# First operands of a hybrid encoder block: the norm chain contiguous, input tiles kept, VectorE in GpSimd's place, units in pairs

## The chip, the cores and the metric

The kernel runs on one core of one Trainium2 chip. The metric is the device time of one execution in microseconds (us), the median of several runs. Engines carry the names of the profile: PE is TensorE, PEld its weight loads, DVE VectorE, ACT ScalarE, POOL GpSimd, SP the engine that issues all DMAs.

## The reference, cut to what matters

One layer, 1024 tokens of width 1024. The piece at the start of the program is `h = rms_norm(x) * (1 + scale) + shift`, where shift and scale come from the vector c by a matrix product, and then `h @ w_in`, a product with many column blocks.

```
shift, scale, gate = adaln(c, w_ada_mix[i], b_ada_mix[i])      # silu(c) @ w + b, split in 3
h = rms_norm(x, norm_mix_w[i]) * (1.0 + scale) + shift
x = x + gate * mixer_sublayer(h, w_in[i], ...)
...
def mixer_sublayer(h, w_in, ...):
    proj = h @ w_in
    conv_in, z, xbc, dt_raw, g_conv, g_ssm = jnp.split(proj, splits, axis=-1)
    a_half, b_half = jnp.split(conv_in, 2, axis=-1)
    u = causal_depthwise_conv(a_half * jax.nn.sigmoid(b_half), conv_dw_w, conv_dw_b)   # 31 taps
    u = jax.nn.silu(layer_norm(u, ...)); y_conv = u @ w_conv_out
    ...                                                        # SSD scan over xbc and dt
    merged = jax.nn.sigmoid(g_conv) * y_conv + jax.nn.sigmoid(g_ssm) * y_ssm
    return merged @ w_out
```

A SwiGLU FFN with a norm of its own and a last norm follow.

## The kernel before

**Layout.** Channels lie on the 128 partitions, tokens along the free dimension. The 1024 tokens are two halves of 512, so a tile is 128x512. Half 0 of h has eight channel tiles `H[0..7]`. Each float32 operand is split in a high part (rounded, ACT) and a low part (the rest, by a subtraction on DVE or POOL), `Hh`/`Hl` and `wh`/`wl`, and each product is three matmuls: high by high, high by low, low by high.

**Start.** `x0` are the eight tiles of half 0. ACT squares them and DVE adds (`SumSq`, names sax and sqx); PE sums over channels (scx, `tokcols`); `rsqrt` makes the reciprocal root r_x in 12 small DVE instructions; `bcast` spreads it over the partitions with matmuls (bx) and an ACT copy (bcx). Beside it `ada` makes shift and scale: for each of eight channel tiles two tiles of 128x1024 (wa_m) are loaded and DVE reduces each against c (an instruction of 1024 columns with a read of the accumulator behind it); `make_h` then multiplies x by gain and root, adds the shift (ACT, `Hh`) and makes `Hl` (DVE).

**Six gates.** `gate0(m)`, m from 0 to 5, are plain products of a weight block with all eight tiles of H: 8 x 3 = 24 matmuls of 512 columns each, into the PSUM tiles p. Gates 0 to 3 run ahead of the step `begin`, gates 4 and 5 behind it.

**Units.** The rest of `proj` is made for both halves at once by a Strassen-Winograd scheme: a unit takes two column blocks, splits seven weight combinations a to g (the splits are named ap0h, ap0l, bp0h, ... by letter and number of the unit), and runs seven products of 12 matmuls each. X is made of a, d, f, g, Y of b, Z of c and e; the PSUM tiles are uXp, uYp, uZp. Its right sides are made from H (half 0) and from the normed tiles of half 1 by `tok_ops`: T1, T2, B22, T3, T4, four tiles of each. That needs the half-1 norm (a second chain scx, r_x, bx, bcx), a scaling of the eight tiles x1t (L883) and whole tiles of h for half 0, which `whole` (L833) adds together again on POOL as Hh + Hl. `Unit.first` runs products a and b, `Unit.rest` c to g. `run_units` decides the order: with A_HEAD = 3 the firsts of units 0, 1, 2, then the rests of 0 and 1, and from there a first and a rest in turn. The table `ENG_A` says for each unit which of its eleven VectorE-like operations go to DVE ("v") and which to POOL ("g"): for unit 0 nine of eleven on DVE, for all others all on POOL.

**Queues.** Instructions are traced in program order and placed by a scheduler; on each engine they run in the order in which they were placed, and a waiting instruction holds up all behind it. `issue_after` forces instructions behind a given one on that one's engine. `tick` feeds background work (31-tap convolutions on DVE as `conv31`, the dt chain `dt_part`) between matmuls. SP issues the DMAs in its own order. `pstile` gives one of four PSUM tiles, `mmtile` one of three, `xtile` one of these or the one in pool cv.

Of the kernel before, what the change touches and what calls it, by code (L numbers as in the profile page):

```python
# [6 lines left out]
F32 = mybir.dt.float32  # L7
# [7 lines left out]
P = 128  # L15
T = 512
# [7 lines left out]
NCK = 4  # L24

NWADA = 8
ROW_AT = 3
A_HEAD = 3
FF_HEAD = 6
FF_TAIL = 2  # L30
G_BOTH = (0, 3)
# [14 lines left out]
N_G0 = 8  # L46
PRI_W = 300

ENG_A = ("ggvvvvvvvvv", "ggggggggggg")
ENG_F = ("vvvvvvvgggg",) * 6 + ("ggvgvgvgvvv",)  # L50
ENG_D = ("vvvvvvvgggg",)
EPS = 1e-6
# [19 lines left out]
def build(tc, ins, outs):  # L72
# [83 lines left out]
    def split_w_(w, ch, nk, eng, alloc=None):  # L156

        parts = []
        for q in range(0, nk, 4):
            n = min(4, nk - q) * P  # L160
            raw = w[:, q * P:q * P + n]
            alloc = alloc or (lambda tag, name: wpool.tile([P, 4 * P], F32R, tag=tag, name=name))
            hi = alloc("whi", f"wh{ch}_{q}")
            act(out=hi[:, :n], in_=raw, func=AF.Copy)  # L164
            lo = alloc("wlo", f"wl{ch}_{q}")
            eng.tensor_tensor(out=lo[:, :n], in0=raw, in1=hi[:, :n].bitcast(F32), op=ALU.subtract)  # L166
            parts.append((hi, lo))
        return parts

    def mm3(out, w, slots, rhs, first=True, last=True, after=None):  # L170

        n = len(slots)
        for i, (s, (rh, rl)) in enumerate(zip(slots, rhs)):
            whi, wlo = w[s // 4]
            sl = slice(s % 4 * P, (s % 4 + 1) * P)
            if i % 2:
                tick()
            ins = after(i) if after else None
            with tc.issue_after(ins) if ins else nullcontext():
# [7 lines left out]
    def xtile(i, name):  # L187

        return pools["cv"].tile([P, T], F32, tag="cv", name=name, bufs=1) if i % 4 == 3 else mmtile(name)
# [74 lines left out]
    def rsqrt(st, scale, eps, name, out=None):  # L264

        v, t = small("v" + name), small("t" + name)
        r = out if out is not None else small("r" + name)
        vec.tensor_scalar(out=v, in0=st, scalar1=scale, scalar2=eps, op0=ALU.mult, op1=ALU.add)
        vec.tensor_scalar(out=r.bitcast(I32), in0=v.bitcast(I32), scalar1=1, scalar2=None,
                          op0=ALU.logical_shift_right)  # L270
        vec.tensor_scalar(out=r.bitcast(I32), in0=r.bitcast(I32), scalar1=-1, scalar2=0x5F3759DF,
                          op0=ALU.mult, op1=ALU.add)
        for _ in range(3):
            vec.scalar_tensor_tensor(out=t, in0=r, scalar=-0.5, in1=r, op0=ALU.mult, op1=ALU.mult)
            vec.tensor_tensor(out=t, in0=t, in1=v, op=ALU.mult)
            vec.scalar_tensor_tensor(out=r, in0=t, scalar=1.5, in1=r, op0=ALU.add, op1=ALU.mult)
        return r

    nrow = [0]
# [54 lines left out]
    def make_h(k, t, gcol, shift, r, eng, dst=H, keep=None):  # L334
        vec.scalar_tensor_tensor(out=t, in0=t, scalar=gcol[:, k:k + 1], in1=r, op0=ALU.mult, op1=ALU.mult)
        hi, lo = dst[k]
        act(out=hi, in_=t, func=AF.Identity, bias=shift[:, k:k + 1])
        if keep is not None:
            act(out=keep, in_=t, func=AF.Identity, bias=shift[:, k:k + 1])
        if eng is vec:  # L340
            vec.scalar_tensor_tensor(out=lo, in0=t, scalar=shift[:, k:k + 1], in1=hi.bitcast(F32),  # L341
                                     op0=ALU.add, op1=ALU.subtract)
        else:
            act(out=t, in_=t, func=AF.Identity, bias=shift[:, k:k + 1])
            gp.tensor_tensor(out=lo, in0=t, in1=hi.bitcast(F32), op=ALU.subtract)

    mod_m = const.tile([P, 24], F32, name="mod_m")
    mod_f = const.tile([P, 24], F32, name="mod_f")
# [527 lines left out]
    def norm_of(b2, r, g, sh, gp_from=KD, fold=False):  # L876

        def scaled(k):
            if k >= gp_from:
                act(out=b2[k], in_=b2[k], func=AF.Copy, scale=g[:, k:k + 1])  # L880
                gp.tensor_tensor(out=b2[k], in0=b2[k], in1=r, op=ALU.mult)
            else:
                vec.scalar_tensor_tensor(out=b2[k], in0=b2[k], scalar=g[:, k:k + 1], in1=r,  # L883
                                         op0=ALU.mult, op1=ALU.mult)
        return scaled, sh, fold
# [259 lines left out]
    def phase_a():  # L1145
        def z_done(i):
            def f(t, src, m, hf):
                act(out=t, in_=src, func=AF.Silu)
                dma(out=z_d[hf, i + m], in_=t)
            return f  # L1150

        def g_done(q, i):
            def f(t, src, m, hf):
                act(out=t, in_=src, func=AF.Tanh, scale=0.5)
                dma(out=gt_d[hf, q, i + m], in_=t)
            return f

        ci = [(CH_CI + 2 * i, CH_CI + 2 * i + 1, ConvIn(i)) for i in range(KD)]
        gates = [((CH_GC, CH_GS)[q] + i, (CH_GC, CH_GS)[q] + i + 1, Each(f"g{q}{i}", g_done(q, i)))
                 for q in range(2) for i in range(0 if q else N_GATE, KD, 2)]  # L1160
        zs = [(CH_Z + i, CH_Z + i + 1, Each(f"z{i}", z_done(i))) for i in range(0, 16, 2)]
        rest = [u for p in zip(gates, zs) for u in p] + zs[len(gates):]
        ssm = [(CH_G + 6 * g + q, CH_G + 6 * g + q + 1, SsmIn(g, q)) for g in G_BOTH for q in range(0, 6, 2)]
        for n, u in enumerate(ssm):
            rest.insert(G_AT + n * G_STEP, u)
        units = []
        while rest or ci:
            if ci and len(units) in CI_AT:
                units.append(ci.pop(0))
            else:  # L1170
                units.append(rest.pop(0))


        def gate0(m):
            def f(w):
                pt = xtile(m, f"p0_0{m}")
                mm3(pt, w, W8, H, after=None if m < 4 else
                    (lambda k: bcast.last if m > 4 or k >= ROW_AT else None))
                t = mp.tile([P, T], F32, tag="x0", name=f"ga{m}", bufs=2)
                act(out=t, in_=pt, func=AF.Tanh, scale=0.5)  # L1180
                dma(out=gt_d[0, 0, m], in_=t)
            step(f, CH_GC + m)

        def begin(_):
            popen("a1", "a1")
            pools.update(u=mp, nev=6, nfr=2, nfs=1)
            pt = [pools["c"].tile([P, NH * T + CW - 1], F32, tag="u", name=f"t1_{k}", bufs=2) for k in range(2)]
            t1 = [pt[k // 2][:, k % 2 * T:(k % 2 + 1) * T] for k in range(4)]
            for _ in tok_ops(pools["a1"], x1t, t1, norm_of(x1t, r_row, gmix, mod_m[:, 0:8])):
                pass  # L1190

        for m in range(4):
            gate0(m)
        step(begin)
        set_drains((bg_dt, 1), (bg_conv_a, CONV_RATE))
        for m in range(4, N_GATE):
            gate0(m)

        def dt1(_):
            bg_dt.append(dt_part(0, ev, [(k, H[k]) for k in range(KD)]))  # L1200

        run_units("p", units, A_HEAD, 0, (False, ()), engs_a, None, {5: [dt1]})


    def phase_b():
# [400 lines left out]

    def xtok(n, k):
        if n == 0:
            t = ap0.tile([P, T], F32, name=f"x0_{k}")
        else:  # L1610
            t = mp.tile([P, T], F32, tag="ev" if k < 6 else "g0", name=f"x1_{k}", bufs=6 if k < 6 else 2)
        dma(out=t, in_=xT[n, :, k, :])
        return t
# [7 lines left out]
        return half_w.pop(0)  # L1621

    def late_w(tag, name):
        return ap0.tile([P, T], F32R, tag="w", name=name, bufs=4)

    x0, x1t = [], []
    ss = SumSq("x0", eng=vec)
# [3 lines left out]
    silu_c(ap0.tile([P, KD * P], F32, tag="wada", name="ctmp", bufs=NWADA))  # L1631
    a = ada(ap0, wada_mix, range(8), mod_m, gmix, "m", True)
    r = bcast(ss.rstd(1.0 / 1024, EPS, out=r_x[0]), "x0", far=False)
    for b in range(KD):
        next(a)
        make_h(b, x0[b], gmix, mod_m[:, 0:8], r, vec)
        if b < 4:
            ch, nk, eng = chunks[b][:3]
            raws.append(load_w_(ch, nk) if b < 2 else ap0.tile([P, 8 * P], F32, name=f"w{ch}"))
            if b > 1:  # L1640
                dma(out=raws[b], in_=wall[ch])
            parts.append(split_w_(raws[b], ch, nk, gp, (None, None, early_w, late_w)[b]))
    ss = SumSq("x1", eng=vec, of=KD)
    for k in range(KD):
        with tc.issue_after(wa_last[0]):
# [108 lines left out]
```

## Time and profile before

| what | value |
|---|---|
| time before, median of 3 runs | 2137.74 us (2136.13 to 2140.61) |
| profiled execution, its own time | 2132.49 us |
| its span, first to last instruction | 2130.5 us |
| PE busy | 1954.8 us, 92% |
| DVE busy | 1561.3 us, 73% |
| POOL busy | 1168.1 us, 55% |
| ACT busy | 964.2 us, 45% |
| mean granted clock | 0.967 |

The profiled execution is 5.2 us under the median, and 2.0 us of it lie outside the span. A busy share is a mean over the whole span; what a stage waits for is read from that stage.

### The profile page before, as it was taken

To read this page: it belongs to the slowest core of one execution; us is meant where nothing else is said; L and a number is where in the kernel's file an instruction comes from. 1 tells how busy PE (TensorE), PEld (TensorE's weight loads), DVE (VectorE), ACT (ScalarE), POOL (GpSimd) and SP (SyncE) were. 2 spreads that over 40 slices of the span, in tenths; PEclk is the share of its full clock that TensorE was granted. 3 is DMA by queue.
4 is the path that set the end of the run, shared out by engine and by line. 5 is a ranking of instruction groups with operands and counts; after the bars stand their busy time and mean duration, and the time that the engine had idled before them with its cause. 6 is when DMAs were issued, how large, how long until landed. Compare 5 with 4: busy or idle time off the path is not lost.

```text
span 2130.5 us, 26723 instructions
## 1 busy us (share of the span) xinstructions
PE 1954.8 (92%) x8802; PEld 1554.5 (73%) x8802; DVE 1561.3 (73%) x2242; ACT 964.2 (45%) x1792; POOL 1168.1 (55%) x871
## 2 busy tenths in 40 slices
PE   4879999999998889898989899998999999989997
PEld 3668678787876666676767677776888888767776
DVE  8868889958899878959779783758644444598645
ACT  3534444444444747446344653346333333444243
POOL 4568678887885854585655764555333333331410
PEclk9889999999999989999999999999999999999998
DMA  8223132322323967689788786863422222576553
GB/s 321 80 70 113 68 102 84 119 104 74 109 102 135 302 201 247 201 301 290 242 277 271 246 260 218 275 229 109 149 99 77 77 84 89 180 255 215 190 187 119
DMA packets 163818, 365.94 MB, mean 172 GB/s; under 512 B 18728, under 2 KB 19168, under 8 KB 163680
## 3 DMA queue, kind: packets, MB, share of 16 engines
q1 hardware_dynamic: 163680, 364.25, 51.2%
q8 instruction: 69, 1.13, 0.2%
q14 instruction: 69, 0.57, 0.1%
HBM read 281.04 MB, written 83.13 MB: 171 GB/s over the span
## 4 chain that ended last, share of the span: by engine, by line
PE 53%; DVE 23%; DMA 13%; issue 4%; ACT 3%; POOL 3%; SPq 1%; DVEq 0%; POOLq 0%; ACTq 0%
PE uXp L805 12%; PE uXf L805 10%; PE uZp L805 6%; PE uZf L805 5%; PE uYp L805 3%; PE uYf L805 2%; DMA M<-acs_d 2%; PE uXd L805 2%; DMA wa_f<-in 2%; DMA yl<-y_d 1%; DVE wa_m L242 1%; DVE wa_f L242 1%; DVE Hl L211 1%; PE uZd L805 1%; PE fd L180 1%
## 5 line engine op out<-in xcount | busy, mean ns | idle before, releaser
L166 POOL TENSOR_TENSOR wl<-w,wh 128x512 fp32r<-128x512 f32 x198 | 283.4, 1440 | 226.6 <-ACT wh L164 185.6
L164 ACT ACTIVATE wh<-w 128x512 fp32r<-128x512 f32 x232 | 136.8, 606 | 135.4 <-DMA w<-in 60.1
L918 POOL TENSOR_TENSOR fw<-fw,fw 128x512 f32<-128x512 f32 x40 | 58.0, 1450 | 117.5 <-DMA fw<-in 116.8
L548 ACT ACTIVATE M<-M,dt_acs 128x128 f32<-128x128 f32 x256 | 81.0, 390 | 45.2 <-DMA M<-acs_d 45.0
L553 POOL TENSOR_TENSOR M<-M,cbm 128x512 f32<-128x512 f32 x48 | 69.4, 1456 | 44.4 <-ACT M L550 25.9
L660 DVE SCALAR_TENSOR_TENSOR pcM<-u,cw_eo,pcM 128x512 f32<-128x512 f32 x120 | 90.3, 752 | 2.7
L660 DVE SCALAR_TENSOR_TENSOR pcQ<-u,pc,pcQ 128x512 f32<-128x512 f32 x112 | 84.4, 754 | 3.0
L182 PE MATMUL s<-Hh,wl 128*128 128x512 f32 x192 | 77.8, 406 | 3.0 <-POOL wl L166 3.0
L660 DVE SCALAR_TENSOR_TENSOR pcR<-u,pc,pcR 128x512 f32<-128x512 f32 x104 | 78.4, 754 | 2.8
L181 PE MATMUL s<-Hl,wh 128*128 128x512 f32 x192 | 77.1, 401 | 2.5 <-DVE Hl L211 2.5
L180 PE MATMUL s<-Hh,wh 128*128 128x512 f32 x192 | 77.3, 406 | 0.5 <-ACT wh L164 0.5
L916 POOL TENSOR_TENSOR fsf<-fw 128x512 f32<-128x512 f32 x22 | 41.2, 1873 | 65.3 <-DVE cf2l L784 10.8
L180 PE MATMUL p<-Hh,wh 128*128 128x512 f32 x144 | 59.0, 430 | 19.1 <-DVE xo L1097 10.8
L180 PE MATMUL p<-Oh,wh 128*128 128x512 f32 x144 | 60.6, 421 | 8.4 <-DVE xo L1097 8.4
L181 PE MATMUL p<-Hl,wh 128*128 128x512 f32 x144 | 60.7, 423 | 5.9 <-DVE Hl L341 5.9
L985 DVE TENSOR_TENSOR s2f<-s2f,uZf 128x512 f32<-128x512 f32 x22 | 15.1, 687 | 62.5 <-PE uZf L805 62.5
L181 PE MATMUL p<-Ol,wh 128*128 128x512 f32 x144 | 60.0, 417 | 0.0
L182 PE MATMUL p<-Oh,wl 128*128 128x512 f32 x144 | 59.5, 414 | 0.0
L925 POOL TENSOR_TENSOR fw<-fw 128x512 f32<-128x512 f32 x40 | 58.6, 1466 | 1.5
L182 PE MATMUL p<-Hh,wl 128*128 128x512 f32 x136 | 56.8, 418 | 0.0
L1094 DVE SCALAR_TENSOR_TENSOR p<-pre,pc,p 128x512 f32<-128x512 f32 x72 | 53.9, 748 | 0.8 <-ACT p L1090 0.2
L180 PE MATMUL wo<-Oh,wh 128*128 128x512 f32 x128 | 51.6, 403 | 0.0
(3620 smaller groups left out, 6973.7 us busy)
## 6 DMA issues: line engine op xcount, KB each, us to landing
fw<-in SPq DMA_DIRECT2D x133, 512.0 KB, 3.4
w<-in SPq DMA_DIRECT2D x100, 512.0 KB, 4.9
M<-acs_d SPq DMA_DIRECT2D x64, 256.0 KB, 6.1
wa_f<-in SPq DMA_DIRECT2D x48, 256.0 KB, 3.5
wa_m<-in SPq DMA_DIRECT2D x16, 512.0 KB, 10.2
xs<-xbc_d SPq DMA_DIRECT2D x32, 256.0 KB, 5.0
E<-eac_d SPq DMA_DIRECT2D x64, 128.0 KB, 6.1
y<-z_d SPq DMA_DIRECT2D x32, 256.0 KB, 5.2
```

Source lines behind the costliest of these rows:

```text
L164: act(out=hi[:, :n], in_=raw, func=AF.Copy)
L166: eng.tensor_tensor(out=lo[:, :n], in0=raw, in1=hi[:, :n].bitcast(F32), op=ALU.subtract)
L180: nc.tensor.matmul(out=out, lhsT=whi[:, sl], rhs=rh, start=first and i == 0, stop=False)
L181: nc.tensor.matmul(out=out, lhsT=whi[:, sl], rhs=rl, start=False, stop=False)
L182: nc.tensor.matmul(out=out, lhsT=wlo[:, sl], rhs=rh, start=False, stop=last and i == n - 1)
L548: act(out=m[:, sl], in_=m[:, sl], func=AF.Relu, scale=-1.0, bias=acs[:, c * 32 + hd:c * 32 + hd + 1])
L553: (gp if e or hf == 0 else vec).tensor_tensor(out=self.M[e], in0=self.M[e], in1=cbm, op=ALU.mult)
L660: vec.scalar_tensor_tensor(out=pt if k < n - 1 else out or pt, in0=src(k), scalar=w(k), in1=pt, op0=ALU.mult, op1=ALU.add)
L805: nc.tensor.matmul(out=out, lhsT=l[:, sl], rhs=r, start=first and k == 0 and i == 0, stop=k == 3 and i == 2, skip_group_check=True)
L918: e[8].tensor_tensor(out=a21, in0=a11, in1=a21, op=ALU.subtract)
L925: e[10].tensor_tensor(out=a12, in0=a12, in1=a11, op=ALU.subtract)
L1094: vec.scalar_tensor_tensor(out=pt, in0=pre[:, k:k + T], scalar=wc(k), in1=pt, op0=ALU.mult, op1=ALU.add)
```

## The change

The change touches the start of the program up to unit 3; what is behind it keeps its code.

- `rsqrt` remembers its last instruction, and from channel tile 1 on the reductions of `ada` and the splits of the first weights are placed behind it.
- The x0 tiles 0 to 3 lie in the lasting tiles `t1f`, 4 to 7 in the convolution's buffers; after `Hl` is made, ACT writes the whole h back into them (`keep`). `tok_ops` takes them from there, and the eight `whole` additions on POOL go.
- `tok_ops` gets DVE as its second engine: four splits B22 and four subtractions of x tiles move from POOL to DVE. It is run in pieces (`more_ops`).
- The weight splits of all six gates move from POOL to DVE; the weights of gates 4 and 5 get buffers of their own and are loaded earlier in SP's queue. The six gates stand ahead of `begin`; gates 4 and 5 take their PSUM tiles from `pstile`.
- `ENG_A` gives units 0 to 3 wholly to DVE, unit 4 and all later ones to POOL as before. A_HEAD is 4: firsts of units 0 to 3, then the rests of 0 and 1 interleaved, then of 2 and 3. Unit 3's X comes from `pstile`.

```diff
-ROW_AT = 3
-A_HEAD = 3
+A_HEAD = 4
...
-ENG_A = ("ggvvvvvvvvv", "ggggggggggg")
+ENG_A = ("vvvvvvvvvvv",) * 4 + ("ggggggggggg",)
...
-            vec.scalar_tensor_tensor(out=r, in0=t, scalar=1.5, in1=r, op0=ALU.add, op1=ALU.mult)
+            rsqrt.last = vec.scalar_tensor_tensor(out=r, in0=t, scalar=1.5, in1=r, op0=ALU.add, op1=ALU.mult).ins
...
         act(out=hi, in_=t, func=AF.Identity, bias=shift[:, k:k + 1])
-        if keep is not None:
-            act(out=keep, in_=t, func=AF.Identity, bias=shift[:, k:k + 1])
         if eng is vec:
             vec.scalar_tensor_tensor(out=lo, in0=t, scalar=shift[:, k:k + 1], in1=hi.bitcast(F32),
                                      op0=ALU.add, op1=ALU.subtract)
...
+        if keep is not None:
+            act(out=keep, in_=t, func=AF.Identity, bias=shift[:, k:k + 1])
...
-                pt = xtile(m, f"p0_0{m}")
-                mm3(pt, w, W8, H, after=None if m < 4 else
-                    (lambda k: bcast.last if m > 4 or k >= ROW_AT else None))
+                pt = xtile(m, f"p0_0{m}") if m < 4 else pstile(f"p0_0{m}")
+                mm3(pt, w, W8, H)
...
-            for _ in tok_ops(pools["a1"], x1t, t1, norm_of(x1t, r_row, gmix, mod_m[:, 0:8])):
-                pass
-
-        for m in range(4):
+            more_ops(tok_ops(pools["a1"], x1t, t1f, norm_of(x1t, r_row, gmix, mod_m[:, 0:8]),
+                             lambda k: x0[k] if k >= 4 else None, vec))
+
+        for m in range(N_GATE):
             gate0(m)
         step(begin)
         set_drains((bg_dt, 1), (bg_conv_a, CONV_RATE))
-        for m in range(4, N_GATE):
-            gate0(m)
...
-        run_units("p", units, A_HEAD, 0, (False, ()), engs_a, None, {5: [dt1]})
+        run_units("p", units, A_HEAD, 0, (False, (3,)), engs_a, None, {5: [dt1]}, True)
...
-            t = ap0.tile([P, T], F32, name=f"x0_{k}")
+            if k >= 4 and k % 2 == 0:
+                xtok.u = pools["c"].tile([P, NH * T + CW - 1], F32, tag="u", name=f"x0_{k}", bufs=2)
+            t = t1f[k] if k < 4 else xtok.u[:, k % 2 * T:(k % 2 + 1) * T]
...
+    r_made = rsqrt.last
     for b in range(KD):
-        next(a)
-        make_h(b, x0[b], gmix, mod_m[:, 0:8], r, vec)
-        if b < 4:
+
+        with tc.issue_after(r_made) if b else nullcontext():
+            next(a)
+        make_h(b, x0[b], gmix, mod_m[:, 0:8], r, vec, H, x0[b])
+        if b < N_GATE:
...
-            parts.append(split_w_(raws[b], ch, nk, gp, (None, None, early_w, late_w)[b]))
+        for i in (b,) if b < 4 else range(4, N_GATE) if b == KD - 1 else ():
+            with tc.issue_after(r_made):
+                parts.append(split_w_(raws[i], *chunks[i][:2], vec, (None, None, early_w, late_w)[min(i, 3)]))
```

How the change moves instructions, at three places. The lines of the changed kernel are one lower up to its L1180, so L274 before is L273 after, L833 is gone, L883 is L882, and L805 is L804.

First place, DVE at the first norm. Before, the root's instructions (L268 to L276) stand between reductions of `ada` (ISA, 128x1024):

```order
L268 TENSOR_SCALAR vx_212<-scx_207 128x4
L269 TENSOR_SCALAR r_x_128<-vx_212 128x4
L271 TENSOR_SCALAR r_x_128<-r_x_128 128x4
L242 ISA wa_m_0_253,gmix<-wa_m_0_253,rw,b1m 128x1024
L242 ISA gmix 128x1
L274 SCALAR_TENSOR_TENSOR tx_213<-r_x_128 128x4
L247 TENSOR_TENSOR gmix<-gmix,pc 128x1
L275 TENSOR_TENSOR tx_213<-tx_213,vx_212 128x4
L242 ISA wa_m_1_256,mod_m<-wa_m_1_256,rw,pc 128x1024
L242 ISA mod_m 128x1
L276 SCALAR_TENSOR_TENSOR r_x_128<-tx_213,r_x_128 128x4
```

Of the change, on DVE at the same place, from the last two of the twelve on:

```order
L274 TENSOR_TENSOR tx_207<-tx_207,vx_206 128x4
L275 SCALAR_TENSOR_TENSOR r_x_128<-tx_207,r_x_128 128x4
L165 TENSOR_TENSOR wl_0_242<-w_238,wh_0_240 128x512
L165 TENSOR_TENSOR wl_4_246<-w_238,wh_4_244 128x512
L241 ISA wa_m_0_248,gmix<-wa_m_0_248,rw,b1m 128x1024
L241 ISA gmix 128x1
L241 ISA wa_m_1_251,mod_m<-wa_m_1_251,rw,pc 128x1024
```

The twelve instructions of the root now stand in a row, and splits of gate weights, once POOL's, stand among the reductions behind them.

Second place, POOL from its first constant on. Before, the splits of the gates and the whole tiles stand there (18 instructions between that constant and the first unit's split, of which the list shows ten):

```order
L376 TENSOR_TENSOR cw_eo<-pc 128x8x15
L166 TENSOR_TENSOR wl_0_247<-w_243,wh_0_245 128x512
L166 TENSOR_TENSOR wl_4_251<-w_243,wh_4_249 128x512
L166 TENSOR_TENSOR wl_0_267<-w_263,wh_0_265 128x512
L166 TENSOR_TENSOR wl_4_271<-w_263,wh_4_269 128x512
L166 TENSOR_TENSOR wh_0_285<-w_283,wh_0_285 128x512
L166 TENSOR_TENSOR wh_4_288<-w_283,wh_4_288 128x512
L833 TENSOR_TENSOR t_0_547<-Hh_103,Hl_104 128x512
L833 TENSOR_TENSOR t_0_547<-Hh_105,Hl_106 128x512
L166 TENSOR_TENSOR wl_0_305<-w_301,wh_0_303 128x512
L166 TENSOR_TENSOR wl_4_309<-w_301,wh_4_307 128x512
```

Of the change, on POOL from the same constant on (u is a convolution's buffer, fw and ap4l are unit 4's weights):

```order
L375 TENSOR_TENSOR cw_eo<-pc 128x8x15
L1066 MEMSET u_965 128x30
L1066 MEMSET u_1247 128x30
L675 TENSOR_TENSOR u_965<-u_965 128x527
L915 TENSOR_TENSOR fsp_1433<-fw_1106 128x512
L783 TENSOR_TENSOR ap4l<-fw_1104,ap4h 128x512
```

Between the constant and the first convolution POOL has only two short memsets left.

Third place, PE at the second norm. Before, the broadcast bx stands right behind the sums scx (the last of them shown), inside gate 4 (p_04):

```order
L257 MATMUL scx_389<-ones,sax_351 128x1
L257 MATMUL scx_389<-ones,sqx_7_387 128x1
L296 MATMUL bx_412<-ident,r_x_129 128x128 x4
L180 MATMUL p_04_681<-Hh_109,wh_0_508 128x512
L181 MATMUL p_04_681<-Hl_110,wh_0_508 128x512
```

Of the change, on PE at bx; between scx and these rows stand 24 matmuls, the products a of units 0 and 1 (uXp_645 and uXp_685), of which the last is shown:

```order
L804 MATMUL uXp_685<-Hh_109,ap1l 128x512
L295 MATMUL bx_434<-ident,r_x_129 128x128 x4
L179 MATMUL p_04_554<-Hh_103,wh_0_357 128x512
L180 MATMUL p_04_554<-Hl_104,wh_0_357 128x512
L181 MATMUL p_04_554<-Hh_103,wl_0_359 128x512
```

All of gates 4 and 5 now stands behind bx, and two products of units ahead of it.

## Rows read from the trace of the kernel before

**Rows 1.** Stretches: length; PE, PEld, DVE, ACT, POOL busy (instructions); clock; DMA share; GB/s.

```profile
0.00:28.10 28.10, 3.91 (x16) 3.56 (x16) 19.99 (x46) 10.99 (x18) 6.79 (x14) 1.00 0.96 354
28.10:63.90 35.80, 25.59 (x84) 18.42 (x85) 35.65 (x45) 12.14 (x21) 17.25 (x10) 0.94 0.58 214
60.00:79.00 19.00, 14.94 (x57) 12.30 (x58) 10.67 (x25) 7.88 (x14) 5.24 (x4) 0.68 0.33 111
134.70:240.00 105.30, 105.21 (x455) 84.96 (x453) 82.70 (x109) 45.38 (x77) 85.02 (x67) 1.00 0.27 90
300.00:600.00 300.00, 298.54 (x1288) 241.21 (x1287) 245.34 (x319) 130.00 (x221) 252.18 (x197) 1.00 0.29 102
600.00:1300.00 700.00, 629.19 (x3160) 491.24 (x3159) 571.77 (x889) 373.85 (x789) 439.41 (x331) 0.95 0.73 238
```

**Rows 2.** Timeline of DVE, first norm to last tile of H.

```profile
17.56 0.16 DVE L268 TENSOR_SCALAR vx<-scx 128x4 f32<-128x4 f32 x1 [0.68 <-PE scx L257]
...
24.93 0.16 DVE L275 TENSOR_TENSOR tx<-tx,vx 128x4 f32<-128x4 f32 x1
25.13 0.16 DVE L276 SCALAR_TENSOR_TENSOR r_x<-tx,r_x 128x4 f32<-128x4 f32 x1
...
57.28 1.27 DVE L242 CUSTOM_DVE_ANT_0 wa_m<-wa_m,rw,b1m 128x1024 f32<-128x1024 f32 x1
...
58.48 1.28 DVE L242 CUSTOM_DVE_ANT_0 wa_m<-wa_m,rw,pc 128x1024 f32<-128x1024 f32 x1
...
63.09 0.75 DVE L341 SCALAR_TENSOR_TENSOR Hl<-x,mod_m,Hh 128x512 fp32r<-128x512 f32 x1
63.75 1.48 DVE L322 TENSOR_TENSOR sax<-sax,sqx 128x512 f32<-128x512 f32 x2
```

**Rows 3.** Timeline of DVE, second norm and operands of units.

```profile
78.31 6.44 DVE L883 SCALAR_TENSOR_TENSOR x<-x,gmix,bcx 128x512 f32<-128x512 f32 x8 [2.80 <-ACT bcx L300]
...
96.16 1.75 DVE L851 TENSOR_TENSOR t<-x,t 128x512 f32<-128x512 f32 x1
97.84 1.77 DVE L211 TENSOR_TENSOR T2l<-t,T2h 128x512 fp32r<-128x512 f32 x1
...
101.22 0.68 DVE L211 TENSOR_TENSOR T2l<-t,T2h 128x512 fp32r<-128x512 f32 x1
101.82 0.68 DVE L873 TENSOR_TENSOR t<-b,t 128x512 f32<-128x512 f32 x1
```

**Rows 4.** Timeline of POOL beside it.

```profile
97.33 1.73 POOL L784 TENSOR_TENSOR bp1l<-fw,bp1h 128x512 fp32r<-128x512 f32 x1
99.02 1.73 POOL L784 TENSOR_TENSOR ap2l<-fw,ap2h 128x512 fp32r<-128x512 f32 x1
102.58 1.67 POOL L833 TENSOR_TENSOR b<-Hh,Hl 128x512 f32<-128x512 f32 x1 [1.83 <-DVE t L873]
```

**Rows 5.** Groups of DVE's instructions by form, 70 to 130 us.

```profile
L851 DVE TENSOR_TENSOR t<-x,t 128x512 f32<-128x512 f32 x8 | 9.5, 1213 | 0.0
L211 DVE TENSOR_TENSOR T1l<-t,T1h 128x512 fp32r<-128x512 f32 x4 | 5.9, 1497 | 0.0
```

**Rows 6.** Timeline of PE: waits, and steps of matmuls at two clocks.

```profile
15.66 1.87 PE L257 MATMUL scx<-ones,sax 128*128 128x1 f32 x8 [15.66 <-DVE sax L322]
...
75.56 2.08 PE L296 MATMUL bx<-ident,r_x 128*128 128x128 f32 x8 [3.46 <-DVE r_x L276]
...
116.18 0.80 PE L805 MATMUL uZp<-T1h,cp0l 128*128 128x512 f32 x1 [5.42 <-DVE cp0l L784]
...
133.34 0.63 PE L805 MATMUL uZp<-B22h,ep0l 128*128 128x512 f32 x1
133.77 0.63 PE L805 MATMUL uZp<-T1h,cp1h 128*128 128x512 f32 x1
...
134.55 0.39 PE L805 MATMUL uXp<-T3h,fp0h 128*128 128x512 f32 x1
...
247.53 1.06 PE L421 MATMUL dt<-Hh,wdhl 128*32 128x512 f32 x2 [3.79 <-DVE wdhl L413]
```

More of the change, by code (lines that the diff above doesn't have):

```diff
@@ L1186, in begin @@
             pools.update(u=mp, nev=6, nfr=2, nfs=1)
-            pt = [pools["c"].tile([P, NH * T + CW - 1], F32, tag="u", name=f"t1_{k}", bufs=2) for k in range(2)]
-            t1 = [pt[k // 2][:, k % 2 * T:(k % 2 + 1) * T] for k in range(4)]
-            for _ in tok_ops(pools["a1"], x1t, t1, norm_of(x1t, r_row, gmix, mod_m[:, 0:8])):
-                pass
-        for m in range(4):
+            more_ops(tok_ops(pools["a1"], x1t, t1f, norm_of(x1t, r_row, gmix, mod_m[:, 0:8]),
+                             lambda k: x0[k] if k >= 4 else None, vec))
+        for m in range(N_GATE):
             gate0(m)
@@ L1623, in late_w @@
     def late_w(tag, name):
-        return ap0.tile([P, T], F32R, tag="w", name=name, bufs=4)
+        return ap0.tile([P, T], F32R, tag="w", name=name, bufs=12)
     x0, x1t = [], []
```

## The prediction, made before the run

> **What bounds the kernel now.** I read the busy shares first, then stretches, then the timelines of the stretches in which PE is not full. From 134.7 to 240 us PE is busy for 105.2 of 105.3 us, from 300 to 600 for 298.5 of 300 [rows 1]. There every matmul that starts earlier ends earlier, and what VectorE (DVE) does beside them is covered. At the start it is the other way round: from 28.1 to 63.9 DVE is busy for 35.65 of 35.80 us and PE for 25.6 [rows 1], and up to 134.55 PE gets through only 254 matmuls of 512 columns (six gates of 24, X and Y of units 0 to 2 with 72, products c, d, e of unit 0 with 36, two of unit 1). At the step of the full stretch, 105.3 / 455 = 0.231 us each [rows 1], these are 59 us of work. So the start is bound by DVE: by the chain norm, scaling, `Hl`, second norm, operands T1 to T4. PE's waits carry DVE's names (r_x, cp0l) [rows 6].
>
> In DVE's queue two things are to be seen. The root takes from 17.56 to 25.29 us, though its last links follow each other by 0.20 us [rows 2]: reductions of 1.20 us stand between them. And the same instruction comes in two lengths: subtractions of two SBUF tiles follow each other by 0.60 us at 101.2, where POOL is idle, and by 1.68 at 96.2, where POOL's instructions follow each other by 1.69 [rows 3, 4]. DVE and POOL take turns there. That holds for whole groups: 1.21 and 1.50 us in the mean for what takes 0.60 alone [rows 5].
>
> The Trainium skill (SBUF — State Buffer, section "SBUF: two separate sides") explains the turns by a port pair that a GpSimd instruction, or a VectorE one with two SBUF inputs, holds for its whole length; by that rule the turns end where GpSimd has no work. Another page (Perfetto Trace Analysis, section "Optimizing Scalar/DVE Operations") speaks against this change: where VectorE is saturated, moving work off to other engines, even GpSimd, may make sense; it adds that the shared port may spoil that. The first rule gives the sum below, the second the slower rival.
>
> **The change, part by part**, along DVE's new queue, with lengths from undisturbed rows.
>
> *Up to the first root*: same instructions, so 17.56 us.
>
> *The root in a row*: 12 x 0.20 = 2.4, ready at 20.0 instead of 25.3.
>
> *Up to the last `Hl`*: the new order has 12 gate splits (0.60 each: 7.2), 14 reductions (1.20: 16.8), 7 small products (I take 0.1: 0.7), 8 scalings and 8 `Hl` (0.66, the step from 63.09 to 63.75 [rows 2]: 10.6), and 6 others of two tiles (3.6). Sum 38.9, end at 58.9 instead of 63.84. The 12 splits, new on DVE, are thus already in. Before, this stretch held less work and took longer. The eight ACT copies that keep h are hidden: ACT is busy for 12.1 of 35.8 us there [rows 1].
>
> *Second norm*: the last-but-one `Hl` stands 1.26 us ahead of the last, at 57.6; from there PE has 12 and 8 gate matmuls, then the sums scx (1.9 [rows 6]), and now 24 unit matmuls ahead of the broadcast bx; from bx to the first scaling of the second half it takes 78.31 - 75.56 = 2.75 [rows 3, 6]. The root itself (2.4) hides beside the 24. At 0.231 us a matmul the scaling starts at T = 57.6 + 4.6 + 1.9 + 5.5 + 2.75 = 72.4; at 0.43, the step at the lower of the two clocks (1.2 instead of 2.4 GHz) [rows 6], at 57.6 + 8.6 + 1.9 + 10.3 + 2.75 = 81.2. Before it was 78.31. Standing behind 24 matmuls is the price of the new order, and PE does useful work in it. Which clock? From 60 to 79 us the granted clock was 0.68 after a stretch in which PE was busy for seven tenths [rows 1]; the new PE is as sparsely fed up to 57 us, but then runs without a pause. I take T = 79, nearer to the low end.
>
> *Operands of the units*: unit 3's product b (uYp<-bp3) has to wait for a PSUM tile, which DVE frees by its 46th instruction from T on (8 scalings at 0.66, 38 of two operands at 0.60): T + 28.1. PE has 108 matmuls up to there, 25 us, so it waits some 4 us. Then 24 matmuls (bp3, cp0), and 254 are done at T + 28.1 + 5.5 = T + 33.6 = 112.6. Before it was 134.55. Gain 21.9; with T at 81.2 it is 19.8, with 72.4 28.5.
>
> *Behind that*: products and their splits come in step. DVE has to split for units 1 to 3 now, 24 instructions or 14.4 us, and idles 22.6 us between 134.7 and 240 [rows 1], so PE covers it. But unit 0's convolution starts 50 matmuls (11.6 us) later in PE's work, since pairs finish together, and the dt chain behind it already holds PE up by 3.79 us in one place [rows 6]. The lengthening lies between 0 and 11.6; I take 2, since the idle time is larger than the added splits. From unit 4 on the code is the same, and a lead is carried through the full stretch up to 600. Interleaving units 2 and 3, and PSUM tiles for gates 4 and 5, cost nothing as long as PE is full; without that cover they would cost a wait on DVE of some 0.6 us for each of 10 splits.
>
> *Transfers*: the same bytes. The weights of gates 4 and 5 go ahead of eight reductions' tiles in SP's queue. Up to the last of these 15.5 MB are asked for; at 354 GB/s, the mean up to 28.1 us [rows 1], they are in at 44 us, and DVE reaches it near 52. Hidden, by 8 us.
>
> Sum: 21.9 - 2 = 19.9 us. The profiled execution would go from 2132.5 to 2112.6; the median shown is 5.2 us above it, and from there I get 2137.7 - 19.9 = **2117.8, say 2118 us**.
>
> **The rivals.**
>
> *The gain is eaten by the convolution and dt.* DVE is busy for 83 of 105 us from 134.7 on [rows 1]; if all of the later start of the convolution shows in the dt chain, 21.9 - 11.6 = 10.3 are left: 2127 us. For it: PE waits for wdhl already. Against: DVE's idle time.
>
> *The middle is put in another order.* Between 600 and 1300 us PE idles for 70.8 us [rows 1], and by the built order some four in ten of the matmuls there stand otherwise than before. A tenth of the idle time is 7 us, either way: 2111 or 2125.
>
> *DVE stays slow, and takes on more.* If the long lengths were DVE's own and not POOL's doing, the 38 instructions behind T would take 1.21 to 1.50 us [rows 5] instead of 0.60: 23 to 34 us more, against 19.9 of gain. That is 3 to 14 us slower, 2141 to 2152. It decides from a mean of 0.60 + 19.9 / 38 = 1.12 us on. For it: all groups there have such means. Against: 0.60 at 101.2 with POOL idle, 1.68 with POOL at work, and in the new order POOL has two memsets up to unit 4. By the rule of the Trainium skill (Perfetto Trace Analysis, section "Optimizing Scalar/DVE Operations") a saturated engine would rather be relieved than loaded; this rival is that case.
>
> *PE keeps its full clock*: T = 72.4, gain 28.5 - 2 = 26.5: 2111 us.
>
> **How the numbers follow.** A difference of 0.2%, 4.3 us, is about what a measurement of this kernel can tell from none. Chances: forecast (gain of 14 to 24 us) 0.55; full clock, or the middle in my favour (gain above 24) 0.17; eaten in part by dt or the middle (gain of 4.3 to 14) 0.15; eaten wholly (within 4.3) 0.06; DVE slow 0.07. So faster 0.87, same 0.06, slower 0.07. The range is from 2107 (full clock, 26.5, and half of what the middle may add) to 2130 (dt takes all that it can, and 3 more); it leaves out two in ten.
>
> **What the profile of the changed kernel would show.** The first root ready at 20 us, the last `Hl` at 59; DVE's two-tile instructions at 0.68 us in all groups up to unit 4, with POOL nearly empty up to some 125 us; bx behind 24 unit matmuls; the scaling L882 from 72 to 81 us; a wait of PE of some 4 us at bp3; product fp0 of unit 0 or its like some 20 us earlier in PE's count of matmuls; 300 to 600 us as full as before. The prediction is wrong if two-tile instructions of DVE stay above 1 us without POOL, if L882 starts later than 85 us, if the waits for wdhl and dt grow by more than 5 us, or if PE's idle time from 600 to 1300 us changes by more than 7.

## The result, and the profile after

The kernel before ran at 2137.3 us (median, 2136.1 to 2140.6), the changed one at **2112.7 us** (2109.5 to 2115.0): ratio 0.988, 95% interval 0.987 to 0.990, 24.6 us faster. The forecast was 2118. The profiled execution went from 2132.5 to 2109.5 us, its span from 2130.5 to 2107.8. (L882 after is L883 before.)

The stretches of the changed kernel, with the columns of [rows 1]:

```profile
28.10:58.90 30.80, 24.35 (x80) 17.68 (x80) 30.80 (x56) 17.15 (x28) 0.00 (x0) 0.94 0.74 284
60.00:79.00 19.00, 19.00 (x97) 15.96 (x96) 13.06 (x30) 11.75 (x20) 0.00 (x0) 1.00 0.45 152
79.00:110.00 31.00, 27.80 (x115) 21.91 (x114) 30.55 (x51) 21.80 (x38) 0.25 (x2) 0.94 0.12 43
134.70:240.00 105.30, 101.14 (x436) 78.69 (x434) 94.56 (x123) 45.01 (x78) 69.04 (x53) 1.00 0.27 92
300.00:600.00 300.00, 297.24 (x1277) 239.02 (x1277) 257.35 (x333) 129.16 (x221) 246.80 (x192) 1.00 0.29 98
600.00:1300.00 700.00, 620.90 (x3121) 481.42 (x3120) 562.16 (x869) 370.81 (x784) 431.95 (x327) 0.95 0.74 241
```

POOL's column is empty from 28.1 to 79 us and all but empty up to 110 (0.25 us), and DVE is still busy for all of the first stretch. From 60 to 79 us PE runs without a pause at a granted clock of 1.00, where before it had 0.68 [rows 1].

The timeline of DVE, for [rows 2, 3], and DVE's groups from 70 to 130 us, for [rows 5]:

```profile
17.75 0.16 DVE L267 TENSOR_SCALAR vx<-scx 128x4 f32<-128x4 f32 x1 [0.68 <-PE scx L256]
...
19.93 0.16 DVE L275 SCALAR_TENSOR_TENSOR r_x<-tx,r_x 128x4 f32<-128x4 f32 x1
20.01 0.69 DVE L165 TENSOR_TENSOR wl<-w,wh 128x512 fp32r<-128x512 f32 x1
...
58.16 0.75 DVE L338 SCALAR_TENSOR_TENSOR Hl<-x,mod_m,Hh 128x512 fp32r<-128x512 f32 x1
...
71.66 5.39 DVE L882 SCALAR_TENSOR_TENSOR x<-x,gmix,bcx 128x512 f32<-128x512 f32 x8 [0.39 <-ACT bcx L299]
...
L850 DVE TENSOR_TENSOR t1f<-x,t1f 128x512 f32<-128x512 f32 x8 | 5.3, 686 | 0.0
L210 DVE TENSOR_TENSOR T1l<-t1f,T1h 128x512 fp32r<-128x512 f32 x4 | 2.6, 686 | 0.0
```

The root is ready at 20.1 us, the last `Hl` at 58.9. Groups that took 1213 and 1497 ns in the mean take 686. The timeline of PE, for [rows 6]:

```profile
62.67 0.28 PE L256 MATMUL scx<-ones,sax 128*128 128x1 f32 x2
...
69.94 1.05 PE L295 MATMUL bx<-ident,r_x 128*128 128x128 f32 x8
...
98.51 0.61 PE L804 MATMUL uXp<-T2h,dp0h 128*128 128x512 f32 x1 [2.76 <-ACT cg L961]
...
99.98 0.80 PE L804 MATMUL uYp<-Hh,bp3h 128*128 128x512 f32 x1 [0.44 <-DVE s1g L984]
...
106.63 0.40 PE L804 MATMUL uXp<-T2h,dp0l 128*128 128x512 f32 x1
```

DVE's scaling starts at 71.66 us, right behind bx. The row at 106.63 is the first matmul behind the 254 that the prediction counts; before, it stood at 134.55 [rows 6]. From 98 to 134.7 us PE waits for 3.2 us in all.

### The profile page after: what moved, and what is told of

It reads as the page before. It is cut to its first block, busy times and chain, and to the rows that moved or that the text cites. A ratio compares the mean times of both kernels' runs of the same rounds, so it can differ in the third digit from the quotient of the medians.

```text
span 2107.8 us, 26688 instructions
## 1 busy us (share of the span) xinstructions
PE 1945.2 (92%) x8802; PEld 1546.2 (73%) x8802; DVE 1564.6 (74%) x2297; ACT 972.2 (46%) x1800; POOL 1074.9 (51%) x808
## 4 chain that ended last, share of the span: by engine, by line
PE 46%; DVE 25%; DMA 17%; issue 5%; POOL 2%; ACT 2%; SPq 1%; DVEq 0%; ACTq 0%; POOLq 0%
PE uXp L804 10%; PE uXf L804 10%; PE uZp L804 5%; PE uZf L804 5%; DMA wa_f<-in 3%; PE uYp L804 2%; PE uYf L804 2%; DMA w<-in 2%; PE uXd L804 2%; DVE gc L1115 2%; DMA yl<-y_d 2%; DVE wa_f L241 1%; DMA M<-acs_d 1%; DVE pcM L659 1%; DVE p L1093 1%
## 5 line engine op out<-in xcount | busy, mean ns | idle before, releaser
L165 POOL TENSOR_TENSOR wl<-w,wh 128x512 fp32r<-128x512 f32 x188 | 269.3, 1442 | 197.5 <-ACT wh L163 188.4
L984 DVE TENSOR_TENSOR s2f<-s2f,uZf 128x512 f32<-128x512 f32 x22 | 15.1, 686 | 61.8 <-PE uZf L804 61.8
L181 PE MATMUL p<-Oh,wl 128*128 128x512 f32 x144 | 58.9, 410 | 0.5 <-POOL wl L165 0.5
L924 POOL TENSOR_TENSOR fw<-fw 128x512 f32<-128x512 f32 x37 | 54.3, 1469 | 1.8
L241 DVE CUSTOM_DVE_ANT_0 wa_f<-wa_f,rw,as_f 128x512 f32<-128x512 f32 x24 | 28.7, 1195 | 33.9 <-DMA wa_f<-in 33.9
```

Source lines behind the costliest of these rows:

```text
L924: e[10].tensor_tensor(out=a12, in0=a12, in1=a11, op=ALU.subtract)
```

## The experiments

A total says little here, since stretches far behind the change move as well. So each profile is also read by PE's count: when the N-th matmul of 512 columns starts (each has 7580), and by how many us that is ahead of the kernel before. N counts from 0, and times from the start of the record; counted from the first instruction, as in the timelines, the figures differ by up to 0.4. Each is one execution. N = 250 is at the end of the first operands, 500 in the full stretch, 4750 to 5500 around the operands of the feed-forward part. The last column is the gain of the medians in us against runs of the kernel before on the same chip.

| kernel | 250 | 500 | 4750 | 5500 | 7500 | gain |
|---|---|---|---|---|---|---|
| the change | 27.3 | 27.7 | 19.8 | 20.7 | 22.7 | 24.6 |
| norm_first | 1.4 | 1.7 | -4.2 | -4.8 | -3.2 | -0.5 |
| dve_for_pool | 28.3 | 27.6 | 22.5 | 29.4 | 30.8 | 35.3 |
| gate_pool | 22.6 | 23.0 | 15.1 | 15.7 | 19.8 | 20.8 |
| no_pairs | 26.4 | 27.1 | 17.6 | 17.6 | 19.1 | 20.6 |
| pool_read | 9.0 | 9.3 | 4.8 | 6.3 | 10.1 | 13.6 (one run) |
| pool_write | 26.3 | 26.7 | 11.5 | 10.7 | 13.2 | 16.7 (one run) |
| whole_pool | 18.5 | 18.9 | 9.1 | 9.7 | 14.2 | 14.4 |
| early_bx | 28.1 | 28.7 | 16.7 | 16.6 | 17.9 | 22.8 |
| dve_start | 27.6 | 26.3 | 16.5 | 17.2 | 22.0 | 29.0 |
| after_ffn | 26.9 | 27.5 | 16.5 | 22.5 | 24.6 | 25.3 |
| dve_norm | 24.6 | 23.7 | 17.4 | 24.3 | 23.1 | 28.6 |
| dve_pair | 27.6 | 27.1 | 24.4 | 26.0 | 28.9 | 29.8 |

**One part alone.** `norm_first` adds only the root in a row to the kernel before; `dve_for_pool` only gives POOL's work to DVE.

```diff
+    r_made = rsqrt.last
     for b in range(KD):
-        next(a)
+        with tc.issue_after(r_made) if b else nullcontext():
+            next(a)
```

> The kernel before with one part of the change alone: the links of the first root follow each other in DVE's queue, the ada reductions stand behind. Theory (POOL's turns are what stretches the start): the root is ready near 20.0 instead of 25.3 us, but the reductions that stood between its links have to be done all the same before the last Hl, and beside POOL's splits DVE is as slow as it was; the last Hl comes between 61 and 64 us, the operands keep their 1.2 to 1.5 us, and the time goes down by 0 to 4 us (2133 to 2138). Rival (the norm chain's place brings the gain): all 5.3 us are carried on and more, since gates start sooner and PE's clock rises sooner: 2122 to 2132.

Measured: 2135.8 us, ratio 1.000 (0.999 to 1.002). No change in the total, 1.4 us at N = 250. DVE and POOL in its timelines:

```profile
18.13 1.19 DVE L271 TENSOR_SCALAR r_x<-r_x 128x4 int32<-128x4 int32 x1
...
20.53 1.18 DVE L274 SCALAR_TENSOR_TENSOR tx<-r_x 128x4 f32<-128x4 f32 x1
21.75 1.18 DVE L275 TENSOR_TENSOR tx<-tx,vx 128x4 f32<-128x4 f32 x1
...
62.90 0.75 DVE L341 SCALAR_TENSOR_TENSOR Hl<-x,mod_m,Hh 128x512 fp32r<-128x512 f32 x1
...
16.59 2.70 POOL L166 TENSOR_TENSOR wl<-w,wh 128x512 fp32r<-128x512 f32 x2 [12.09 <-ACT wh L164]
20.43 2.48 POOL L166 TENSOR_TENSOR wl<-w,wh 128x512 fp32r<-128x512 f32 x2 [1.14 <-ACT wh L164]
```

Even links of 128x4, 0.16 us elsewhere, take 1.18 beside POOL's four splits, so the root comes at 23.1 us and not at 20. The last `Hl` ends at 63.65, before at 63.84 [rows 2]: moving the root only changed the order inside a stretch that DVE fills.

```diff
-ENG_A = ("ggvvvvvvvvv", "ggggggggggg")
+ENG_A = ("vvvvvvvvvvv",) * 4 + ("ggggggggggg",)
...
-            gp.tensor_tensor(out=t, in0=H[k][0].bitcast(F32), in1=H[k][1].bitcast(F32), op=ALU.add)
+            vec.tensor_tensor(out=t, in0=H[k][0].bitcast(F32), in1=H[k][1].bitcast(F32), op=ALU.add)
...
-            for _ in tok_ops(pools["a1"], x1t, t1, norm_of(x1t, r_row, gmix, mod_m[:, 0:8])):
+            for _ in tok_ops(pools["a1"], x1t, t1, norm_of(x1t, r_row, gmix, mod_m[:, 0:8]), None, vec):
...
-            parts.append(split_w_(raws[b], ch, nk, gp, (None, None, early_w, late_w)[b]))
+            parts.append(split_w_(raws[b], ch, nk, vec, (None, None, early_w, late_w)[b]))
```

(and the splits of gates 4 and 5 likewise)

> The kernel before with the other part alone: everything that POOL did in the first operands and in units 0 to 3 is given to DVE (gate weight splits, sums Hh+Hl, the splits B22, the T3 differences, the units' splits); order of the norm, no kept tiles, three units ahead, no pairs, as before. Theory: DVE's two-tile instructions fall to a step of 0.60 to 0.70 in all groups up to unit 4; the 38 instructions of the operands gain 23 to 34 us, some 20 added ones of 0.60 cost 12; the lead over the kernel before at 254 matmuls is 10 to 22 us, and the time 2115 to 2128. Rival (DVE is the bound by its load): the lengths stay above 1.1 us, every instruction that is added costs, and it is slower than 2141.

Measured: 2100.0 us, ratio 0.983 (0.980 to 0.986): the fastest kernel of the study. Its lead at N = 250 is 28.3, the changed kernel's 27.3. So giving POOL's work to DVE is enough for the whole gain of the start. DVE is also the faster of the two at such an instruction; the next two runs ask what POOL's work costs DVE by itself. The lead came out above the expected 10 to 22, and the time below the expected 2115; why the total is shorter than that of the change is taken up below.

**POOL's reads or POOL's work.** Both kernels are the changed one with 21 instructions on POOL from the second bcx on; the second has 20 memsets in place of the additions.

```diff
+    scr = tmp("scr")
+    gp.tensor_tensor(out=scr, in0=r_row, in1=r_row, op=ALU.add)
+    for _ in range(20):
+        gp.tensor_tensor(out=scr, in0=scr, in1=r_row, op=ALU.add)      # pool_write: gp.memset(scr, 1.0)
```

> The changed kernel and, from the second broadcast row on (71.6 us), 21 additions of two 128x512 SBUF tiles on POOL whose result nobody uses. Theory (POOL and DVE take turns on two-tile work): each of the 21 stands between two instructions of DVE, whose step goes from 0.60 to near 1.69 for as long as POOL works; 21 x 1.08 = 23 us at most, the products cp0 end 12 to 23 us later than at 106.8, and the time goes up by 8 to 23 us, to 2120 to 2136. Rival (lengths are DVE's own, or set by what DVE reads): nothing changes, 2113.

> The same place with one addition and 20 memsets of the same 128x512 tile on POOL, which read no tile. If turns are taken only where POOL reads tiles from SBUF, DVE keeps its 0.60 and the time stays at 2113; if any work of POOL that writes to SBUF takes a turn, it goes as with the 21 additions, 2120 to 2136.

Measured: 2122.3 and 2119.2 us, one run each. The timelines, `pool_read` (POOL and DVE):

```profile
73.20 27.03 POOL L1653 TENSOR_TENSOR scr<-scr,bcx 128x512 f32<-128x512 f32 x16
...
72.03 13.55 DVE L882 SCALAR_TENSOR_TENSOR x<-x,gmix,bcx 128x512 f32<-128x512 f32 x8 [0.39 <-ACT bcx L299]
85.51 3.48 DVE L850 TENSOR_TENSOR t1f<-x,t1f 128x512 f32<-128x512 f32 x2
...
103.71 0.68 DVE L850 TENSOR_TENSOR t1f<-x,t1f 128x512 f32<-128x512 f32 x1
```

and `pool_write` (POOL and DVE):

```profile
72.69 11.63 POOL L1653 MEMSET scr<- 128x512 f32 x20
...
71.55 6.27 DVE L882 SCALAR_TENSOR_TENSOR x<-x,gmix,bcx 128x512 f32<-128x512 f32 x8 [0.39 <-ACT bcx L299]
77.74 1.28 DVE L850 TENSOR_TENSOR t1f<-x,t1f 128x512 f32<-128x512 f32 x2
```

Beside POOL's additions DVE and POOL both step by 1.69 us (13.55 / 8, 27.03 / 16); when POOL is done, the same L850 takes 0.68. Beside 20 memsets DVE steps by 0.60 (1.28 for two), and only the one addition ahead of them costs a turn (6.27 against 5.39 for eight). The lead at N = 250 falls from 27.3 to 9.0 with reads, and to 26.3 with memsets. Of the 21 additions 17 fall before 100.3 us; at 1.09 us each (1.69 - 0.60) they make 18.5 us, and 18.3 are lost. The Trainium skill (SBUF — State Buffer, section "SBUF: two separate sides") limits the lock of a VectorE instruction with two SBUF inputs to GpSimd operations that read SBUF; these two traces agree, 1.69 against 0.60 us. The totals of the two runs lie only 3 us apart and would not have told reads from memsets: `pool_write` gains 7.9 us less than the change, and its start explains 1.0 of them. The table shows that it lost the others between N = 500 and 4750, in code that both kernels share; why is not known.

**Parts taken back from the change.** `gate_pool` puts the gates' splits on POOL again (`gp` for `vec` in `split_w_`), `whole_pool` leaves the kept tiles unused so that POOL makes the eight sums, `no_pairs` has A_HEAD = 3 and no pairs, `early_bx` forces product a of unit 1 behind bx.

> The changed kernel with the twelve weight splits of the six gates back on POOL. Theory: each of them that meets DVE's two-tile work makes one DVE instruction take 1.68 instead of 0.60, so 12 splits save DVE 7.2 us and cost it up to 13; the last Hl comes 0 to 6 us later than 58.9, and the time goes up by 0 to 6 us (2113 to 2119). Rival (load): 7.2 us of DVE work less in a stretch that DVE bounds, the last Hl near 52 us, 2106 us.

Measured: 2114.5, ratio 0.990 (0.988 to 0.993). The last `Hl` on DVE:

```profile
62.36 0.75 DVE L338 SCALAR_TENSOR_TENSOR Hl<-x,mod_m,Hh 128x512 fp32r<-128x512 f32 x1
```

It ends 4.2 us later than in the changed kernel (63.1), and the lead at N = 250 is smaller by 4.7. Relieving DVE of twelve instructions made it later.

> The changed kernel with the kept input tiles unused: the eight sums Hh+Hl are made by POOL again, four at 58 us and four near 95. Theory: four of them meet DVE's idle time near 61 to 71 us and cost nothing, four meet the last operands and cost DVE up to 1.08 us each; 0 to 4 us, 2113 to 2117. Rival (POOL's work is harmless): no change at 2113.

Measured: 2121.5, ratio 0.994 (0.992 to 0.996), more than expected, since four of the sums fall not behind the last `Hl` but in DVE's full stretch, from 31.7 to 50.2 us. DVE beside three of them:

```profile
32.76 1.76 DVE L334 SCALAR_TENSOR_TENSOR t1f<-t1f,gmix,bcx 128x512 f32<-128x512 f32 x1
...
35.70 1.24 DVE L246 TENSOR_TENSOR gmix<-gmix,pc 128x1 f32<-128x1 f32 x1
...
42.41 2.31 DVE L241 CUSTOM_DVE_ANT_0 wa_m<-wa_m,rw,pc 128x1024 f32<-128x1024 f32 x1
```

In the changed kernel these forms take 0.75, 0.15 and 1.28 us. A turn costs some 1.0 to 1.1 us whatever DVE's instruction is, and four of them are the 4.0 us by which the last `Hl` is later (62.9). The lead at N = 250 is 8.8 us smaller, so as much again comes behind it: PE gets through 23 matmuls from 45 to 60 us at a granted clock of 0.73 (45 at 0.89 in the changed kernel) and starts the sums scx 6.2 us later, and the last two sums of POOL take their turns from 97.8 us on.

> The changed kernel with the first units in the order of before: three ahead instead of four, and products c to g unit by unit instead of in pairs. Theory: DVE's pace sets the start; without unit 3's 24 matmuls ahead, PE waits for cp0 and its successors by up to 24 x 0.23 = 5.5 us, and gets back what unit 0's earlier end gives the dt chain (0 to 3 us): 2111 to 2118. Rival (the order of the units is a main part of the gain): most of the lead of 28 us at 254 matmuls is lost, 2122 or more.

Measured: 2114.7, ratio 0.990 (0.988 to 0.993). Lead at N = 250: 26.4. The order in pairs is worth a microsecond at the start and no total that can be told.

> The changed kernel with product a of unit 1 put behind the second broadcast, so that bx has 12 unit matmuls ahead of it instead of 24. The root is ready at 66.9 us, so bx can start at 67.2 instead of 69.9, and the scaling at 69 instead of 71.7. PE waits for only 3.2 us in all between 98 and 106 us, which bounds the gain: 0 to 3 us, 2110 to 2113. Rival (other products then come later, and the second wait moves to them): no gain, or 1 to 3 us lost.

Measured: 2113.1, ratio 0.989 (0.987 to 0.990). The scaling starts at 69.4 instead of 71.7, the lead at N = 250 is 0.8 larger, the total the same. Twelve of the 24 matmuls ahead of bx, moved away, change the total by nothing that can be measured.

**Why the trial with DVE in POOL's place is faster still.** Its gain is 10.7 us larger than that of the change. Of this, 6 us show between N = 4750 and 5500, where its row gains 6.9 us and the changed kernel's 0.9; the rest shows before N = 4750 and in the medians, and is not explained. The edit of `whole` also holds for four sums in the feed-forward part, which the change leaves on POOL. The three largest waits of PE from 1405 to 1490 us (waiting tile, releaser: us in total, times, longest) in the changed kernel:

```profile
PE uZf L804 <- DVE B22l L210: 5.3, 1, 5.3
PE uZf L804 <- DVE g L984: 3.3, 2, 1.9
PE bx1f L295 <- DVE r_x L275: 1.5, 1, 1.5
```

and what DVE does ahead of the first of them:

```profile
1462.89 1.73 DVE L872 TENSOR_TENSOR t1f<-b,t1f 128x512 f32<-128x512 f32 x1 [2.45 <-POOL b L832]
1464.55 1.74 DVE L783 TENSOR_TENSOR ef1l<-fw,ef1h 128x512 fp32r<-128x512 f32 x1
1466.21 3.46 DVE L210 TENSOR_TENSOR B22l<-b2f,B22h 128x512 fp32r<-128x512 f32 x2
```

It is the start once more: DVE waits 2.45 us for a sum of POOL and then takes turns with it. `dve_start` gives these four sums of `dve_for_pool` back to POOL, `after_ffn` takes them from POOL in the changed kernel.

> The first trial with DVE in POOL's place (2100 us) was also given to the four sums Hh+Hl of the second feed-forward operands, far behind the start; here those four are on POOL again and all else is as in that trial. Theory: they were worth the 8 to 9 us by which that trial moved ahead between the 4750th and the 5000th matmul, where the changed kernel waits 5.3 us for B22l behind POOL's sum; so 2106 to 2110, with a lead of 28 at the 250th matmul and 20 to 23 at the 5000th. Rival (the start is better by itself, or the order of the middle): it stays at 2100.

Measured: 2105.6 (2096.9 to 2110.5), ratio 0.986 (0.983 to 0.989). Between N = 4750 and 5500 it gains 0.7 us.

> The changed kernel with the same four sums of the second feed-forward operands on DVE. Theory: DVE has no more wait for POOL's sum there and its splits B22l take 0.60 instead of 1.7; the wait of 5.3 us at uZf and that of 1.5 at bx1f go, 5 to 9 us in all: 2104 to 2108. Rival: DVE, with four instructions more, is late elsewhere in the same stretch, no change at 2113.

Measured: 2109.3 (2105.4 to 2115.9), ratio 0.988 (0.986 to 0.991). Between N = 4750 and 5500 it gains 6.0 us, and PE's largest waits there are

```profile
PE uZf L804 <- DVE g L984: 4.0, 2, 3.8
PE uXf L804 <- DVE s5f L984: 1.2, 1, 1.2
```

The waits for B22l and r_x are gone. The change and `dve_start`, with the sums on POOL, gain 0.9 and 0.7 us in this stretch, `dve_for_pool` and `after_ffn`, with the sums on DVE, 6.9 and 6.0; the seven other kernels with them on POOL lie between -0.8 and 1.5. So the place of the sums is shown to matter. The wait for B22l is not its only form: in `dve_start` it is missing, and PE waits there for T2l (2.3 us) and s5f (2.2) instead; at N = 5000 it is 4.7 us further ahead than at 4750, and 4.0 of them are gone at 5500. In the total of `after_ffn` this doesn't arrive: its median is 3.3 us below that of the change, inside the spread of its runs, and its gain on its own chip larger by only 0.7; its profile lost more between N = 500 and 4750.

> The first trial with DVE in POOL's place and the links of the first root in a row as well, i.e. the two parts that were run alone, together. Theory: with POOL silent the stretch up to the last Hl is DVE's work from end to end, so the order in it changes the end by less than 2 us: root at 20 instead of 28, last Hl within 2 us of 56.3 to 57.1, 2099 to 2102. Rival (the norm's place counts once POOL no longer covers it): the root's 8 us are carried on, 2092 to 2096.

Measured: 2106.0, ratio 0.987 (0.985 to 0.988): 6 us slower than `dve_for_pool` by the medians, 6.7 by the gains, and outside both expectations. Two stretches, `dve_for_pool` first and `dve_norm` behind it:

```profile
28.10:45.00 16.90, 12.75 (x44) 9.91 (x45) 16.90 (x31) 5.32 (x9) 0.00 (x0) 1.00 1.00 388
45.00:60.00 15.00, 14.01 (x60) 10.78 (x59) 14.76 (x27) 7.84 (x14) 0.00 (x0) 1.00 0.22 72
```

```profile
28.10:45.00 16.90, 12.53 (x39) 8.95 (x39) 16.90 (x30) 4.34 (x7) 0.00 (x0) 1.00 1.00 388
45.00:60.00 15.00, 10.12 (x34) 7.47 (x35) 14.90 (x27) 7.46 (x12) 0.00 (x0) 0.77 0.23 73
```

The early root lets PE start sooner but thinly: from 45 to 60 us 34 matmuls instead of 60, with a granted clock of 0.77 instead of 1.00. The sums scx then start at 64.5 instead of 60.6 us, the scaling at 71.1 instead of 67.2, and at N = 500 it is 3.9 us behind. The last `Hl` accounts for 1.7 us of this; how the other 2 divide between matmuls left over and the clock was not separated.

> The first trial with DVE in POOL's place, and the eight weight sums of the first two feed-forward units on DVE as well. In that trial POOL makes them from 1434 to 1446 us, while DVE's two-tile instructions beside them take 1.6 to 1.8, and PE waits 3.2 us for g and 0.3 again. Theory: DVE gives 8 x 0.60 = 4.8 us and gets back some 7 x 1.1 = 7.7, PE's waits there go down by 0 to 4 us: 2096 to 2100. Rival (load): the added 4.8 us make PE wait longer, 2101 to 2105.

Measured: 2104.8, ratio 0.986 (0.984 to 0.988). Not faster than `dve_for_pool`; its runs (2101.4 to 2106.5) overlap those (2098.4 to 2103.2). Between N = 4750 and 5500 it gains 1.6 us where `dve_for_pool` gains 6.9, and PE's two largest waits there are

```profile
PE uZf L805 <- DVE cf1l L784: 4.1, 1, 4.1
PE uXf L805 <- DVE df1l L784: 2.6, 1, 2.6
```

This is the rival's case: PE waits for work that DVE was given in addition.

## Why the prediction came out

*What bounds the start, and the turns*: right. Reads of POOL stretch DVE, memsets don't, and POOL's work given to DVE alone gives the lead. The rival that DVE is slow by itself falls with 686 ns, and the thought behind it, that a full DVE should be relieved, with `gate_pool`.

*The root and the last `Hl`*: forecast at 20.0 and 58.9 us, found at 20.1 and 58.9. But the reading of the root was incomplete. The text put its lateness down to the reductions between its links; in the kernel before, three links were themselves stretched, beside POOL, two of them here:

```profile
20.36 1.25 DVE L274 SCALAR_TENSOR_TENSOR tx<-r_x 128x4 f32<-128x4 f32 x1
...
21.65 1.18 DVE L275 TENSOR_TENSOR tx<-tx,vx 128x4 f32<-128x4 f32 x1
```

With the order alone (`norm_first`) the root comes at 23.1 us, so of the 5.3 us the order has 2.2, and the other 3 come from POOL's silence. And the root in a row has next to no share in the gain: alone it gives 1.4 us at N = 250 and nothing in the total, and on top of DVE in POOL's place it costs some 4 us at N = 500. The sum of DVE's work was right; that the root's place in it mattered was not.

*T, the start of the scaling*: mis-sized. The text took "T = 79, nearer to the low end", between 72.4 at full clock and 81.2; it was 71.66, with a granted clock of 1.00 from 60 to 79 us. The 24 matmuls ahead of bx took 0.23 us each. The text took PE to be as sparsely fed up to 57 us as before. It was not: from 45 to 60 us PE was busy for 12.4 of 15 us, before for 10.6. In the changed kernel the granted clock was 0.89 in these 15 us and 1.00 from 60 on; in the kernel before it was 0.98 and then, from 60 to 65 us, 0.50. This is the rival "PE keeps its full clock".

*Operands*: T + 28.1 for the PSUM tile of bp3 gives 99.8; PE went on there at 99.98. Instead of a wait of 4 us at bp3 there were 2.76 at the product before it and 0.44 at bp3. The 254 matmuls were done at 106.6, T + 35.0 (forecast T + 33.6). The gain at that point is 27.9 us, forecast 21.9, and 28.5 for full clock.

*Convolution and dt*: 2 us were taken, none came. At N = 500 and 1000 the lead is 27.7 and 28.5. PE's waits from 134.7 to 300 us are 2.7 + 1.0 for dt, and a new one of 2.8 at uXp; before they were 3.8 + 0.4, and 3.4 at acs.

*The middle*: from 600 to 1300 us PE idles for 79.1 us (700 - 620.9), before for 70.8, so 8.3 more, above the 7 that the text set as its limit. The wait that grew most is that of the matmuls sc for DVE's ry, from 6.5 to 14.2 us; it is 9 to 14 us in all kernels with units in pairs and 5.5 to 6.6 in the others, but 13.2 in `norm_first`, which has no pairs, so the pairs are not shown to be its cause. The lead goes from 27.7 at N = 500 to 19.8 at 4750. All thirteen kernels of the table lose 3 to 15 us there against this one profile of before, `norm_first` 5.9 without any gain to lose; and the profiled execution of before lies 4.8 us under its median (2132.5 against 2137.3), that of the change 3.2. So part of this is probably the spread of single executions; by the medians 3 of the 27.7 us are lost. Why the middle costs some kernels more than others stays open.

So 24.6 us instead of 19.9: 6 us more from the clock and 2 from dt, and some of it lost again in the middle. The forecast held to 5 us partly by luck, because two errors had opposite signs. A gain above 24 us was the case to which the text gave 0.17, for full clock or a favourable middle, and 2112.7 lies nearer to the 2111 of the rival "PE keeps its full clock" than to the forecast: the stage that the change aimed at was understood, the clock behind it was not.

## What to carry to other kernels

Before moving work to an idle POOL, price each of its instructions that reads SBUF at one turn of DVE (here 1.0 to 1.1 us), not at nothing: where DVE is full, DVE does such work cheaper itself (0.60 us), and where it has no slack either, as in `dve_pair`, it doesn't pay. Look for the same pattern elsewhere in the program before tuning its first place further: four sums 1400 us later were worth some 6 us in their stretch, more than the root's place, the pairs or an earlier bx. And judge an edit of one stage by PE's count at the end of that stage; totals here move by several microseconds for reasons that lie elsewhere.

## What was not expected of the hardware

- A turn costs DVE about the same whatever it runs: a product of 128x1 took 1.24 instead of 0.15 us, a reduction of 1024 columns 2.31 instead of 1.28 (`whole_pool`). An integer instruction of 128x4 with a single SBUF input took 1.19 instead of 0.17 (`norm_first`), so it isn't instructions with two inputs alone that wait.
- A thinner start of PE, sooner, came with a lower granted clock from 45 to 60 us (0.77 against 1.00), and its work ended later than that of a PE that waited for 10.8 us at the first root's broadcast, against 3.0, and then ran densely (`dve_norm` and `dve_for_pool`, one execution each).
